# A hybrid decoder step on one core: the down product of two slices as seven chained rounds, ahead of the third

## The chip, the core and the metric

The kernel runs on one core of a Trainium2 chip. The core has a matrix engine (TensorE, PE in the profile, with its weight loads as PEld), VectorE (DVE), ScalarE (ACT), GpSimd (POOL) and SyncE (SP), which only issues transfers; POOL issues transfers too. The metric is the device time of one execution in microseconds (us).

## The reference

One inference step of a two-layer decoder over 1104 tokens (64 sampled, 16 meta, 1024 prompt tokens) of width 1024, all in float32. Layer 0 mixes with an mLSTM, layer 1 with an attention; behind each stands the same kind of feed-forward network:

```python
def swiglu(xn, w_gu, w_d):
    gu = xn @ w_gu
    return (jax.nn.silu(gu[..., :D_FF]) * gu[..., D_FF:]) @ w_d
...
        h = h + swiglu(rmsnorm(h, prm['norm_ffn'][l]), prm['w_gate_up'][l], prm['w_down'][l])
        if l == N_A_LAYERS - 1:
            shared = shared_kv(h, prm['norm_kv'], prm['w_kvf'], prm['b_fg_b'], prm['k_norm_b'])
    y = rmsnorm(h, prm['norm_final'])
```

`D_FF` is 2816. The change is in the last product, `@ w_d`, the down product, in both layers.

## The kernel before

**Tiling.** Activations lie with features on the 128 partitions and tokens along the free side. The 1104 tokens are three slices of 368 (`t` = 0, 1, 2). The residual is `H[t]`, 8 feature tiles of 128x368. The inner features are 22 tiles of 128 (`NF`), taken as 11 pairs (`NC`, `c`). Every float32 product is made of three matmuls: operands are split into a high part (a cast to fp32r on ScalarE) and a low part (a subtraction on VectorE), and high x high, high x low and low x high are summed in PSUM. `split` (L330 to L332) does a split.

**Gate and up.** `Unit` makes the gate (even `x`) or up (odd `x`) product of two feature tiles. `mark` (L1491, L1492) combines partial products from PSUM on VectorE; `out` multiplies silu(gate) by up (L1534) and sends each of the six results of an odd unit (two feature tiles, three slices) to DRAM, `hT[t]`, on SP (L1535). TensorE's order is written by hand here, that of the other engines is the scheduler's. The names `s1`, `c15`, `s2`, `e`, `t4`, `v2` are 128x368 columns in SBUF that hold an odd unit's results until they are sent.

**Down.** The last unit and the down product run with the orders of TensorE, VectorE and ScalarE written by hand; SP's and POOL's are the scheduler's. The product is a list of steps, `seq`: for each slice `t`, each half `z` of the output features (512 columns) and each pair `c`, one step of 24 matmuls of 128x368 (four output tiles `m`, two feature tiles, three products). Four PSUM banks (`dps`) hold the four outputs; behind the 11th pair they are added to `H[t]` (`add`, L1491).

A step needs a weight block (two tiles by 512 columns, 512 KB) and a pair of activations (368 KB). `w_load(i + 5)` fetches weights on SP into one of three raw buffers (`slots[0]`, `slots[1]`, `wr`), `w_split(i + 2)` splits them into one of four places (`slots[2 + i % 4]` and its low part). `h_load` fetches a pair from `hT` on POOL, through `flat[0]` and `flat[2]` at first and then through three buffers `hr`; `h_split` splits it into a place in the tiles `x0`, `x1`, `x2` and `T`, where it stays for the second half. `H[t]` itself is fetched back from DRAM (`hD`, 1472 KB) on POOL during the product, since its memory (`flat`, named `vA` in layer 0 and `Ht` in layer 1) is a buffer until then.

Behind a slice's outputs come squares (ScalarE) and their sum (`add_sq`, POOL L405, the last on VectorE), and then the norm: in layer 0 `norm_x`, which makes the inputs of the keys and values, in layer 1 `final`, the result. They are generators, taken a piece per step during the next slice's matmuls. Only slice 2's stands behind the last step. In layer 0 `first_values` then makes the first values, tile by tile.

Of the kernel before, what the change touches and what calls it, by code (L numbers as in the profile page):

```python
# [7 lines left out]
F32 = mybir.dt.float32  # L8
# [8 lines left out]
P = 128  # L17
D = 1024
KT = D // P
# [233 lines left out]
class Net:  # L253
# [139 lines left out]
    def add_sq(self, H, t, m, sp, x, late=KT - 1):  # L393
# [4 lines left out]
        if x == 0:  # L398
            self.sums[t] = self.ns[:, t % 2, :n]
            nc.scalar.activation(self.sums[t], H[t][:, m], AF.Square)  # L400
            return
# [77 lines left out]
    def mlp(self, H, w, l, heads=None, cb=None, early=None):  # L479
# [4 lines left out]
        self.sums = {}  # L484
# [3 lines left out]
        with self.pool(self.uid("nsp")) as sp, self.pool(self.uid("npp"), bufs=2, space=PSUM) as pn:  # L488
# [116 lines left out]
            with cw if not cb else ExitStack():  # L605
                def each(t, m):
                    if cb or t < 2 or m < KT - 2:
                        self.add_sq(H, t, m, sp, m)
# [5 lines left out]
                if cb:  # L614
                    def after(t):
                        nc.gpsimd.dma_start(self.hD[:, :, TS[t][0] : TS[t][1]], H[t])
                        return self.norm_x(H, t, None, sp, pn, psum=t < 2)
# [847 lines left out]
def ffn(self, H, flat, l, weights, order, mix, small, each, after, end, early=None):  # L1465
# [8 lines left out]
    hT = [self.dram.tile([P, NF, SL], F32, name=f"hT{l}_{t}") for t in range(3)]  # L1474
    with self.pool(f"ffn{l}") as fp, self.pool(f"ffnp{l}", space=PSUM) as pp:
# [19 lines left out]
        class Unit:  # L1495
# [34 lines left out]
            def out(u, c, i, t):  # L1530

                o = u.c[c]
                if u.odd:
                    tt(out=o, in0=o, in1=keep[t, i], op=ALU.mult)  # L1534
                    nc.sync.dma_start(hT[t][:, u.f + i], o)  # L1535
                else:
                    nc.scalar.activation(o, o, AF.Silu)
                    keep[t, i] = o

# [52 lines left out]
            def tail(u):  # L1592
# [15 lines left out]
        seq = [(t, z, c) for t in range(3) for z in range(2)  # L1608
               for c in ((*range(1, NC), 0) if (t, z) == (2, 1) else range(NC))]

        hseq = [i for i, (t, z, c) in enumerate(seq) if z == 0 or (t, c) == (2, 0)]
        hraw, hpart, wraw, wpart = {}, {}, {}, {}

        def h_load(j):
            if j < len(hseq):
                t, z, c = seq[hseq[j]]
                n = size[t]
                y, o = ((flat[0], 0), (flat[0], 2 * SL), (flat[2], 0), (flat[2], 2 * SL))[j] if j < 4 else (
                    self.ny(f"hr{l}_{j}"), 0)
                hraw[j] = y[:, o : o + 2 * n].rearrange("p (k n) -> p k n", k=2)  # L1620
                nc.gpsimd.dma_start(hraw[j], hT[t][:, 2 * c : 2 * c + 2])  # L1621

        def h_split(j):
            if j < len(hseq):
                t, z, c = seq[hseq[j]]
                x0, x1, x2 = (cut(self.flat_x[y], n) for y, n in ((0, 3), (1, 4), (2, 4)))
                a = [y for x in (2, 1, 4) for y in cut(Tx[x], 2)] + x2
                y = a[2] if z else [x0 + x1 + a[:4], a[4:] + x1 + a[:1], a[1:] + a[:1] + a[1:2]][t][c]
                hpart[t, c] = tuple(p[:, : 2 * size[t]].rearrange("p (k n) -> p k n", k=2) for p in y)
                self.split(hraw.pop(j), *hpart[t, c])  # L1630

        view = lambda y: y[:, : KT * P].rearrange("p (k n) -> p k n", k=2)

        def w_load(i):
            if i < len(seq):
                t, z, c = seq[i]
# [1210 lines left out]
```

## Time and profile before

| | us |
|---|---|
| median of 3 runs | 2843.36 (2842.17 to 2843.45) |
| profiled execution | 2841.83 |
| its span | 2840.1 |
| mean granted TensorE clock | 0.996 of full speed |

Each time below is from that one execution, counted from the start of its span. A row of the order of time has start, duration, engine, line, operation, output<-inputs and, in brackets, how long the engine had stood idle before it and what ended that. A row of busy time by stretch has the stretch, its length, the busy time (instructions) of PE, PEld, DVE, ACT and POOL, the granted clock, the busy share of the DMA engines and GB/s. Some matmul records are missing, so counts in a stretch can be a few per cent low.

### The profile page before, as it was taken

Reading aid. Unit: us, or ns where it says so; the run is one execution under the profiler, and the core shown is the slowest. Engines: PE = TensorE matmul, PEld = TensorE weight load, DVE = VectorE, ACT = ScalarE, POOL = GpSimd, SP = SyncE. Lnnn points to the kernel's source line nnn. Section 1 sums busy time; section 2 is a strip of 40 time slices with the busy share of each in tenths; the row PEclk is TensorE's granted clock in tenths of the full one; section 3 lists DMA queues with packets and bytes.
Section 4 is the critical chain, followed back from the end, with each engine's and each line's share of the span. In section 5 each row is a group of like instructions: output and inputs, shape, how many; then the busy total and the mean of one; then the engine's idle time right before and its main releaser. Section 6 shows DMA issues by size and latency. Waiting matters only on the chain. (4 is left out here: it accounts for less than half of the span.)

```text
span 2840.1 us, 54146 instructions
## 1 busy us (share of the span) xinstructions
PE 2773.6 (98%) x20630; PEld 2651.7 (93%) x20630; DVE 1743.6 (61%) x3606; ACT 1318.1 (46%) x2636; POOL 1085.0 (38%) x1582
## 2 busy tenths in 40 slices
PE   8999998999999999999999999999999999999999
PEld 7997988999999999999999888777999999999998
DVE  6144566687787755553466543777478777775553
ACT  6122464444444434443345444877344454443432
POOL 3042333066656411117572202555307666631210
PEclk9999999999999999999999999999999999999999
DMA  7156664122222275644453676442413222236653
GB/s 218 29 139 166 164 182 156 53 89 77 82 85 79 94 267 194 207 156 142 132 174 120 238 289 221 135 171 88 159 50 91 78 78 90 77 109 243 214 191 106
DMA packets 313974, 399.81 MB, mean 141 GB/s; under 512 B 28966, under 2 KB 235794, under 8 KB 312690
## 3 DMA queue, kind: packets, MB, share of 16 engines
q1 hardware_dynamic: 277282, 277.66, 30.8%
q0 software_dynamic: 35680, 118.12, 12.9%
q8 instruction: 162, 2.65, 0.4%
q14 instruction: 98, 0.80, 0.1%
q10 hardware_dynamic: 752, 0.57, 0.1%
HBM read 299.50 MB, written 96.77 MB: 140 GB/s over the span
## 5 line engine op out<-in xcount | busy, mean ns | idle before, releaser
L332 DVE TENSOR_TENSOR slot<-slot,slot 128x1024 fp32r<-128x1024 f32 (+3 forms) x263 | 252.6, 962 | 117.2 <-ACT slot L331 111.8
L331 ACT CAST slot<-slot 128x1024 fp32r<-128x1024 f32 (+3 forms) x263 | 206.5, 787 | 227.9 <-PE dps L270 95.9
L1515 PE MATMUL m<-x0h,slot 128*128 128x368 f32 x640 | 178.3, 329 | 0.0
L1515 PE MATMUL m<-x1h,slot 128*128 128x368 f32 x640 | 174.1, 331 | 2.7 <-DVE ns L1492 0.9
L1621 POOL DMA_DIRECT2D hr<-hT x60 | 32.5, 541 | 271.9 <-DVE T_2l L332 68.1
L111 POOL TENSOR_TENSOR slot<-vA 128x256 f32<-128x256 f32 x80 | 75.4, 952 | 149.8 <-DMA vA<-in_w_gate_up 77.6
L111 POOL TENSOR_TENSOR slot<-Ht 128x256 f32<-128x256 f32 x80 | 75.1, 949 | 150.3 <-DMA Ht<-in_w_gate_up 78.6
L1515 PE MATMUL m<-x2h,slot 128*128 128x368 f32 x480 | 132.3, 330 | 0.0
L332 DVE TENSOR_TENSOR slot<-Ht,slot 128x256 fp32r<-128x256 f32 (+3 forms) x101 | 88.1, 874 | 56.3 <-ACT slot L331 56.3
L332 DVE TENSOR_TENSOR slot<-vA,slot 128x256 fp32r<-128x256 f32 (+3 forms) x101 | 88.1, 874 | 55.4 <-ACT slot L331 55.4
L1515 PEld LDWEIGHTS m<-x1h,slot 128*128 128x128 f32 x640 | 115.6, 188 | 4.6 <-DVE vA L1491 1.5
L1515 PEld LDWEIGHTS m<-x0h,slot 128*128 128x128 f32 x640 | 116.1, 188 | 0.0
L405 POOL TENSOR_TENSOR ns<-ns,nq 128x368 f32<-128x368 f32 x50 | 56.6, 1133 | 142.5 <-ACT nq L403 136.5
L1515 PE MATMUL m<-x1l,slot 128*128 128x368 f32 x320 | 105.6, 330 | 0.0
L1515 PE MATMUL m<-x0l,slot 128*128 128x368 f32 x320 | 105.5, 330 | 0.0
L2641 ACT ACTIVATE s<-s,nb 128x272 f32<-128x272 f32 (+7 forms) x126 | 98.8, 786 | 0.0
L2676 ACT COPY th<-tp 128x768 f32<-128x768 f32 (+1 forms) x80 | 73.6, 921 | 47.4 <-PE tp L2668 25.8
L1515 PE MATMUL m<-T_2h,slot 128*128 128x368 f32 x320 | 93.8, 334 | 0.4 <-ACT vA L1521 0.4
L1515 PE MATMUL m<-T_4h,slot 128*128 128x368 f32 x320 | 93.7, 334 | 0.0
L326 DVE SCALAR_TENSOR_TENSOR slot<-slot,gain,slot 128x256 fp32r<-128x256 f32 (+2 forms) x152 | 63.7, 466 | 43.5 <-ACT slot L325 41.1
L332 DVE TENSOR_TENSOR slot<-wr,slot 128x1024 fp32r<-128x1024 f32 x42 | 53.5, 1274 | 60.0 <-ACT slot L331 60.0
L1515 PEld LDWEIGHTS m<-x2h,slot 128*128 128x128 f32 x480 | 86.9, 188 | 0.0
(867 smaller groups left out, 10362.3 us busy)
## 6 DMA issues: line engine op xcount, KB each, us to landing
slot<-in_w_down SPq DMA_DIRECT2D x88, 512.0 KB, 4.6
hr<-hT POOLq DMA_DIRECT2D x60, 368.0 KB, 5.4
wr<-in_w_down SPq DMA_DIRECT2D x42, 512.0 KB, 3.8
wraw<-in_w_in_a SPq DMA_DIRECT2D x40, 512.0 KB, 4.2
vA<-in_w_gate_up SPq DMA_DIRECT2D x40, 512.0 KB, 4.1
Ht<-in_w_gate_up SPq DMA_DIRECT2D x40, 512.0 KB, 4.2
kp<-in_cache_k SPq DMA_DIRECT2D x32, 512.0 KB, 5.9
vp<-in_cache_v SPq DMA_DIRECT2D x32, 512.0 KB, 8.4
```

The source lines that it names most:

```text
L111: self.net.nc.gpsimd.tensor_tensor(out=o, in0=a, in1=b, op=op)
L326: nc.vector.scalar_tensor_tensor(out=lo[:, k], in0=raw[:, k], scalar=gk, in1=hi[:, k].bitcast(F32), op0=ALU.mult, op1=ALU.subtract)
L331: self.nc.scalar.copy(hi, src)
L332: self.nc.vector.tensor_tensor(out=lo, in0=src, in1=hi.bitcast(F32), op=ALU.subtract)
L405: (nc.vector if x >= late else nc.gpsimd).tensor_tensor(out=s, in0=s, in1=sq, op=ALU.add)
L1515: nc.tensor.matmul(u.b[b][:, :SL], w[p][:, k], x[q][:, k], start=new and k == i == 0, stop=k == 1 and i == 2, skip_group_check=True)
L1621: nc.gpsimd.dma_start(hraw[j], hT[t][:, 2 * c : 2 * c + 2])
L2641: nc.scalar.activation(ss[z, u], ss[z, u], AF.Exp, bias=nb[:, z : z + 1], accum_out=sm[:, u, z : z + 1])
L2676: nc.scalar.copy(th.rearrange("p x z (u h q) -> p h (x z u) q", h=2, q=64)[:, :, :n], pt[:, :, :n])
```

## The change

Ten of the eleven pairs of slices 1 and 2 are taken as a two by two block product: the two slices are its columns, the two output halves its rows, and the first and second tile-group of the pairs (`h` = 0, 1) what is summed over. Seven products (`round_`) of five steps each take the place of eight. Their activations are `hA[1]` to `hA[7]`: 1, 2 and 4 are plain results of `out`, and 5, 6, 3 and 7 are made by `combine`, four sums per odd unit on VectorE. Their weights are plain for rounds 2, 3 and 6 (6 takes the sum that round 1 left) and sums on VectorE for 5, 1, 7 and 4 (`w_sum`, 20 per layer). Two weight halves are kept in the tiles `x1` and `x2` (`keep_w`, named `wx`). The first pair of slices 1 and 2 remains plain. The rounds are chained: an accumulator is added to several outputs, and the next round goes on in it. Then slice 0 follows with 22 plain steps, each activation pair split once for both halves, in reversed order for the second.

```diff
-    hT = [self.dram.tile([P, NF, SL], F32, name=f"hT{l}_{t}") for t in range(3)]
+    hT = [self.dram.tile([P, NF if t == 0 else 2, SL], F32, name=f"hT{l}_{t}") for t in range(3)]
+    hA = {r: self.dram.tile([P, NF // 2 - 1, SL], F32, name=f"hA{l}_{r}") for r in range(1, 8)}
...
-                    nc.sync.dma_start(hT[t][:, u.f + i], o)
+                    if t == 0:
+                        nc.sync.dma_start(hT[0][:, u.f + i], o)
+                    elif (t, i) != (2, 0):
+                        u.send({(1, 0): 1, (1, 1): 2, (2, 1): 4}[t, i], c)
...
+            def combine(u, part=None):
+
+                for r, o, i, j, f in (((5, "v2", "t4", "e", add),), ((6, "c15", "v2", "s2", sub), (3, "s1", "s1", "c15", sub)),
+                                      ((7, "e", "s2", "e", sub),))[part]:
+                    f(u.c[o], u.c[i], u.c[j])
+                    u.send(r, o)
...
+        def plain(t, z, lead):
+            step(("p", 0, z, 1), ("p", t, 0, 0), lead, (t, z))
+
+        round_(2, True)
+        plain(1, 0, False)
+        plain(2, 0, True)
+        round_(5, True, (2, 1))
+        round_(3, False)
+        plain(1, 1, False)
+        plain(2, 1, True)
+        round_(1, True, (1, 0))
+        round_(6, False, (1, 1))
+        round_(7, False, (2, 0), (2, 1))
+        round_(4, True, (2, 0))
...
+                if 3 <= i < 3 + NR:
+                    keep_w(1, i - 3, 0, 0)
+
+        def w_sum(i):
+            if i < len(ws) and ws[i][0] == "r":
+                _, r, q = ws[i]
+                if r == 5:
+                    sub(kept[1, q], wraw[i], kept[1, q])
+                    wraw[i] = kept[1, q]
+                elif r == 1:
+                    sub(kept[1, q], kept[2, q], kept[1, q])
+                elif r == 7:
+                    sub(wraw[i], kept[2, q], wraw[i])
+                elif r == 4:
+                    sub(wraw[i], wraw[i], kept[1, q])
...
+            for g in range(3):
+                u.combine(g)
...
+                k, todo = min(i + 2, len(seq) - 1), None
+                while wj < wneed[k]:
+                    wj += 1
+                    w_split(wj)
+                    todo = wj
+                while hj < hneed[k]:
+                    hj += 1
+                    h_split(hj)
+                    h_load(hj + 3)
+                if todo and not out:
+                    w_sum(todo + 1)
...
+                    for t, z in out:
+                        y = H[t][:, 4 * z + m]
+                        add(y, y, o)
...
+                if todo and out:
+                    w_sum(todo + 1)
+                if todo:
+                    w_load(todo + 3)
...
-    for t in range(3):
+    n = 0
+    for t in (1, 2, 0):
```

In `final` the slice that stands last is now slice 0, and the buffers of the results of slices 1 and 2 are new tiles.

**SP, at the start of the down product of layer 0.** Before, from the fourth weight block on (`slot` and `wr` are raw weight buffers, `hT` the sends of the last odd unit):

```order
L1638 DMA slot_4927<-in_w_down 128x2x512
L1535 DMA hT_1_5875<-vA_85 128x368
L1535 DMA hT_0_5874<-vA_83 128x368
L1535 DMA hT_2_5876<-nr_4921 128x368
L1535 DMA hT_0_5874<-vA_85 128x368
L1638 DMA slot_4928<-in_w_down 128x2x512
L1535 DMA hT_1_5875<-vA_85 128x368
L1535 DMA hT_2_5876<-vA_85 128x368
L1638 DMA wr_10025<-in_w_down 128x2x512
```

The same place now (`wx` are kept blocks; L1708 loads the block of the plain steps 5 and 6, the `wr` of the fourth row is step 3's):

```order
L1693 DMA wx_10177<-in_w_down 128x2x512
L1537 DMA hT_0_5874<-vA_85 128x368
L1693 DMA wx_10106<-in_w_down 128x2x512
L1545 DMA hA_1_5877<-vA_85 128x368
L1716 DMA wr_10102<-in_w_down 128x2x512
L1545 DMA hA_5_5881<-vA_83 128x368
L1545 DMA hA_6_5882<-vA_85 128x368
L1545 DMA hA_3_5879<-vA_85 128x368
L1545 DMA hA_7_5883<-vA_85 128x368
L1693 DMA wx_10106<-in_w_down 128x2x512
L1708 DMA slot_4928<-in_w_down 128x2x512
L1693 DMA wx_10106<-in_w_down 128x2x512
```

Kept blocks and the four combined sends now stand between the weight blocks of the first steps.

**POOL, at the same place.** Before (`hr` are pairs, `vA<-hD` the three slices of H, 83 to 85 for slice 0 to 2):

```order
L1621 DMA hr_6_10093<-hT_0_5874 128x736
L1851 DMA vA_83<-hD 128x8x368
L1621 DMA hr_7_10124<-hT_0_5874 128x736
L1851 DMA vA_84<-hD 128x8x368
L1621 DMA hr_8_10156<-hT_0_5874 128x736
L1621 DMA hr_9_10187<-hT_0_5874 128x736
L1851 DMA vA_85<-hD 128x8x368
```

Now (pair 5 and 6 are those of the plain steps 5 and 6):

```order
L1669 DMA hr_5_10114<-hT_1_5875 128x736
L1669 DMA hr_6_10150<-hT_2_5876 128x736
L1969 DMA vA_83<-hD 128x8x368
L1969 DMA vA_84<-hD 128x8x368
L1669 DMA hr_7_10184<-hA_5_5881 128x736
L1669 DMA hr_8_10216<-hA_5_5881 128x736
L1969 DMA vA_85<-hD 128x8x368
L1669 DMA hr_9_10247<-hA_5_5881 128x736
```

The three loads of H keep their places, but slices 1 and 2 are now added to in steps 5 and 6, where before slice 0 was the first, in step 10.

**VectorE, at the end of a group of rounds in layer 0.** Before, at the end of the first half of slice 0 (L1491 with `dps` adds an accumulator to H, L332 is the low part of a split):

```order
L332 TENSOR_TENSOR slot_4932<-wr_10025,slot_4931 128x1024
L1491 TENSOR_TENSOR vA_83<-vA_83,dps_10030 128x368
L1491 TENSOR_TENSOR vA_83<-vA_83,dps_10037 128x368
L1491 TENSOR_TENSOR vA_83<-vA_83,dps_10044 128x368
L1491 TENSOR_TENSOR vA_83<-vA_83,dps_10051 128x368
L332 TENSOR_TENSOR slot_4930<-slot_4927,slot_4929 128x1024
```

Now, where round 7 ends and round 4 begins (L1493 is a weight sum, L1492 an addition into H, x2 for two output halves):

```order
L1493 TENSOR_TENSOR slot_4928<-slot_4928,wx_10106 128x1024
L405 TENSOR_TENSOR ns_4920<-ns_4920,nq_10101 128x368
L332 TENSOR_TENSOR slot_4932<-slot_4928,slot_4931 128x1024
L332 TENSOR_TENSOR x0l_5421<-hr_33_11105,x0h_5420 128x736
L1492 TENSOR_TENSOR vA_85<-vA_85,dps_10745 128x368 x2
L1492 TENSOR_TENSOR vA_85<-vA_85,dps_10752 128x368 x2
L1492 TENSOR_TENSOR vA_85<-vA_85,dps_10759 128x368 x2
L1492 TENSOR_TENSOR vA_85<-vA_85,dps_10766 128x368 x2
L1493 TENSOR_TENSOR wr_10102<-wr_10102,wx_10106 128x1024
L332 TENSOR_TENSOR slot_4926<-wr_10102,slot_4925 128x1024
L332 TENSOR_TENSOR x0l_5421<-hr_34_11139,x0h_5420 128x736
```

A weight sum now stands directly ahead of the split of the same block, and eight additions where four stood.

189 lines of the change are left out of this document (122 added, 67 removed).

## The prediction

> **What bounds the kernel now.** I read the page's busy table first, then the busy time by stretch inside the down products (layer 0 from about 1000 to 1266, layer 1 from about 2560 to 2829).
>
> ```profile
> span 2840.1 us, 54146 instructions
> PE 2773.6 (98%) x20630; PEld 2651.7 (93%) x20630; DVE 1743.6 (61%) x3606; ACT 1318.1 (46%) x2636; POOL 1085.0 (38%) x1582
> ...
> core 0: us, PE busy (x) PEld busy (x) DVE busy (x) ACT busy (x) POOL busy (x), PEclk, DMA share, GB/s
> 1010.50:1095.10 84.60, 84.60 (x506) 84.60 (x505) 39.51 (x39) 32.28 (x39) 13.81 (x20) 1.00 0.62 215
> 1095.10:1179.00 83.90, 83.90 (x500) 83.66 (x500) 46.54 (x57) 38.87 (x51) 11.06 (x17) 1.00 0.55 184
> 2577.00:2660.00 83.00, 83.00 (x498) 83.00 (x496) 40.56 (x40) 34.27 (x40) 12.85 (x17) 1.00 0.56 188
> ```
>
> TensorE is busy 98% of the span, and in the three stretches inside the down products it is busy in every microsecond at a granted clock of 1.00, while VectorE works about half of the time. So each matmul taken out of these stretches is worth its interval, as long as nobody makes TensorE wait. The interval, from two rows of the order of time in TensorE (the first and the 25th matmul of one step, 24 apart):
>
> ```profile
> 1010.63 0.33 PE L269 MATMUL dps<-x1h,slot 128*128 128x368 f32 x1
> ...
> 1014.65 0.33 PE L269 MATMUL dps<-x1h,slot 128*128 128x368 f32 x1
> ```
>
> One row lasts 0.33 us, but they overlap: 4.02 us for 24, or 0.1675 us each. A step (one pair of weight tiles, four outputs, 24 matmuls) takes 4.02 us. The row at 1010.63 is step 3 of layer 0 (the first three pairs lie in x0, the fourth in x1), so step 0 began near 998.6.
>
> **Term 1, the matmuls.** Before: 3 slices x 2 halves x 11 pairs = 66 steps per layer. After: 7 rounds x 5 + 4 plain + 22 = 61. Five steps, 120 matmuls x 0.1675 = 20.1 us per layer, 40.2 us in both. That is all the change can give.
>
> **Term 2, the start of the rounds.** The stretch is already bound by transfers:
>
> ```profile
> 1005.00:1010.00 5.00, 5.00 (x32) 5.00 (x31) 1.63 (x2) 0.11 (x1) 1.44 (x2) 1.00 1.03 394
> 1010.00:1015.00 5.00, 5.00 (x32) 5.00 (x31) 2.06 (x2) 2.50 (x3) 0.55 (x1) 1.00 1.03 383
> 1030.00:1035.00 5.00, 5.00 (x32) 5.00 (x31) 2.75 (x3) 2.86 (x3) 0.54 (x1) 1.00 0.97 344
> 1040.00:1045.00 5.00, 5.00 (x31) 5.00 (x31) 3.55 (x6) 2.89 (x5) 1.43 (x2) 1.00 0.00 0
> ...
> 1009.89 1.05 ACT L331 CAST slot<-wr 128x1024 fp32r<-128x1024 f32 x1 [5.17 <-DMA wr<-in_w_down]
> 1010.97 1.23 DVE L332 TENSOR_TENSOR slot<-wr,slot 128x1024 fp32r<-128x1024 f32 x1 [4.34 <-ACT slot L331]
> 1012.12 0.92 DVE L332 TENSOR_TENSOR x1l<-hr,x1h 128x736 fp32r<-128x736 f32 x1
> ...
> vA<-hD POOLq DMA_DIRECT2D x6, 1472.0 KB, 9.6
> ```
>
> From 1005 to 1035 the DMA share is about 1 at some 385 GB/s, and only at 1040 is it idle. The cast of step 5's weights waits for its transfer; both low parts are ready at 1012.12 + 0.92 = 1013.0, and step 5 begins at 998.6 + 5 x 4.02 = 1018.7. So TensorE is about 5.7 us ahead of trouble there, and call it 5 for the whole stretch.
>
> Into this stretch the change puts five kept weight blocks (5 x 512 KB = 2.62 MB, read beside rounds 2 and 5) and three more sends of 184 KB (0.57 MB); one weight load goes, as the two plain steps share theirs (0.52 MB). Net 2.67 MB / 0.385 MB per us = 6.9 us. VectorE gets the last pair's four sums there:
>
> ```profile
> 1040.03 0.54 DVE L1491 TENSOR_TENSOR vA<-vA,dps 128x368 f32<-128x368 f32 x1 [4.40 <-PE dps L271]
> 1043.06 0.54 DVE L1491 TENSOR_TENSOR vA<-vA,dps 128x368 f32<-128x368 f32 x1 [0.48 <-PE dps L271]
> 1043.52 3.14 DVE L332 TENSOR_TENSOR slot<-slot,slot 128x1024 fp32r<-128x1024 f32 x2
> ```
>
> An operation of 128x368 lasts 0.54 us: four are 2.2, and the four additions into H, which now come in step 5 and not in step 10, are as much. They queue in VectorE behind the splits for two steps later, and the next steps need the accumulators that they read. Lateness: 6.9 + 2.2 + 2.2 - 5 = 6.3; I take **+6 us per layer**. Ends: 0 if the lead grows to 11 us, since a stall can't be less than nothing; 12 if the 1472 KB of H for slice 2, which has to wait for a pair buffer, also comes late (a rival below). On SP, the sends wait for VectorE's sums, and behind them stand the second kept block and the weights of step 5; on POOL, H of slice 2 stands behind two pair loads.
>
> **Term 3, the weight sums.** In rounds 5, 1, 7 and 4 each step has a new order: sum (VectorE), cast (ScalarE), low part of the weights, low part of the pair (VectorE), next sum. Each waits for the one before it:
>
> ```profile
> 1014.15 1.05 ACT L331 CAST slot<-slot 128x1024 fp32r<-128x1024 f32 x1 [2.50 <-DMA slot<-in_w_down]
> 1015.23 1.23 DVE L332 TENSOR_TENSOR slot<-slot,slot 128x1024 fp32r<-128x1024 f32 x1 [2.20 <-ACT slot L331]
> 1016.38 0.92 DVE L332 TENSOR_TENSOR x1l<-hr,x1h 128x736 fp32r<-128x736 f32 x1
> ...
> 1044.54 2.96 POOL L405 TENSOR_TENSOR ns<-ns,nq 128x368 f32<-128x368 f32 x2 [1.37 <-ACT nq L403]
> ```
>
> No row shows the f32 sum of 128x1024. Nearest is the split's subtraction of that size (1.23 us); bounds are the 736 columns of the pair (0.92) and the pair of splits beside POOL's additions (3.14 / 2 = 1.57). I take 1.23, as the size is the same. Then: sum to cast 1.23 + 0.06, cast to low part 1015.23 - 1014.15 = 1.08, low part to the next 1.15, that to the sum 0.9 (0.92 with a little overlap): 4.4 us against TensorE's 4.02. With idle time of VectorE inside it, a step is 0.35 us too slow: rounds 5 and 1 are five steps each and followed by rounds without sums, which let it recover (0). Rounds 7 and 4 follow one another: ten steps, 3.5 us. Within them come the additions of round 6's end (4) and of round 7's end (8, two per accumulator); the rows at 1043.06 and 1043.52 are 0.46 apart: 12 x 0.46 = 5.5. POOL's additions of slice 1's squares fall into the same steps, and VectorE lost 3.14 - 2 x 1.15 = 0.84 us beside them; six times 0.75 is 4.5. Sum 13.5. There are four buffers for split weights, and a split writes the one that TensorE left four weights ago, so VectorE can be two steps (8 us) ahead when round 7 begins: 5.5, so **+6 us per layer**, mostly between round 7 and round 4, where TensorE needs accumulators whose additions stand behind splits. Ends: 1 (POOL's additions fall into VectorE's idle time, sums of 0.92) and 10 (the lead is one step).
>
> **Term 4, the clock.** What a stall costs beyond itself stands in the gate/up product:
>
> ```profile
> 599.49 0.56 PE L1515 MATMUL m<-U_6h,slot 128*128 128x368 f32 x1 [1.98 <-DVE vA L1491]
> ...
> 596.00:600.00 4.00, 2.02 (x11) 1.71 (x11) 4.00 (x7) 2.68 (x5) 3.92 (x5) 0.96 0.55 167
> 600.00:604.00 4.00, 4.00 (x18) 4.00 (x16) 4.00 (x3) 0.00 (x0) 4.00 (x4) 0.62 0.45 131
> 604.00:608.00 4.00, 4.00 (x25) 4.00 (x25) 2.25 (x5) 1.00 (x3) 2.72 (x3) 1.00 0.01 2
> ```
>
> After a wait of 1.98 us the clock was 0.62 over the next 4 us, 18 matmuls and not 24 or 25: (1 - 0.62) x 4 = 1.5 us lost. Terms 2 and 3 hold one such stall each: **+3 us per layer** (0 if they come as many short ones, 5 if there are three). The Trainium skill, page "TensorE: Matmul & The Clock Gate", section "Part 1: The HAM clock gate", says that the clock is halved after at least one idle window of about 3.4 us; by that rule stalls of 2 or 3 us cost nothing more, and the time would be 6 us lower. The rows above do not agree with so long a window, and the sum goes by them.
>
> **Term 5, gate and up.** The four sums of each odd unit (40 per layer) and three more sends lie beside matmuls:
>
> ```profile
> 804.00:844.80 40.80, 40.80 (x245) 40.53 (x244) 32.25 (x52) 19.81 (x42) 24.97 (x25) 1.00 0.26 80
> ...
> 726.70 0.54 DVE L1492 TENSOR_TENSOR ns<-m,ns 128x368 f32<-128x368 f32 x1
> 727.92 0.54 DVE L1491 TENSOR_TENSOR ns<-m,ns 128x368 f32<-128x368 f32 x1 [0.68 <-PE m L1515]
> ...
> L1534 DVE TENSOR_TENSOR Ht<-Ht,Ht 128x368 f32<-128x368 f32 x18 | 15.5, 862 | 0.0
> ```
>
> Two units take 40.8 us, of which VectorE works 32.25. Four sums are 2.2 us alone and 3.4 at the 862 ns that such products take beside POOL, so it stays under 36. Two of them stand ahead of the subtraction at 726.70 that frees a bank: it comes 0.9 us later, and VectorE waited 0.68 us for TensorE after it. So up to 0.2 us per even unit: **+1 us per layer** (0 to 4). Sends: 80 GB/s leave room.
>
> Nothing else is on the path: ScalarE's 8 more casts per layer have room (32.28 of 84.60 us busy). The slices' new order at the end leaves the same number of tiles and transposes behind the last step (0, within 1 us either way); the values start with slice 1, whose norm was done earlier, just as slice 0's was.
>
> **Sum.** Per layer -20.1 + 6 + 6 + 3 + 1 = -4.1; both -8.2. The profiled execution took 2841.83 us (span 2840.1 and 1.7 around it), the median of the three runs is 1.5 above it: 2833.6 beside the profile, **2835.2** as a median.
>
> **The rivals.**
> 1. *All is hidden.* Terms 2 to 4 at their lower ends (0, 1, 0), gate/up 1: 2 x (-20.1 + 2) = -36, 2807. For it: VectorE works only 40 to 47 of 84 us in the down product, and a lead of 5 us exists in the worst stretch. Against: the DMA share of 1.03 and the chain of 4.4 us. 17%.
> 2. *The losses eat the gain, and no more.* Each layer loses 17 to 23 us: 2838 to 2849. It needs 4 us more than the forecast in each layer, for instance VectorE one step less ahead at round 7 (term 3 at 10). 28%.
> 3. *Slower: H of slice 2.* Its transfer stands in POOL behind two pair loads, of which the second needs the buffer that step 5's split frees. In the forecast that split ends near 1019, and at the 9.6 us above H lands near 1029, for an addition due at 998.6 + 6.25 x 4.02 = 1023.7. If it lands after 1036, TensorE stands 7 us longer and has another cold clock: 1.5. Then -4.1 + 8.5 = 4.4 per layer, 2852. It decides from about 1036 on. For it: three loads of H and the kept blocks share one saturated DMA. Against: the 9.6 us. 17%.
> 4. *The change does not do what it says*: excluded, as 240 matmuls fewer stand in TensorE's order (17001 rows and 16761).
>
> **How the numbers follow.** Forecast (2825 to 2837.6) 38%; rival 1 17%, rival 2 28%, rival 3 17%. A measurement of this kernel can tell about 0.2%, 5.7 us, from no change. Faster by more: 38 + 17 = 55%; within: 28%; slower: 17%. The range 2813 to 2853 leaves out half of rival 1 and a part of rival 3. The forecast's own range is 2825 to 2838.
>
> **What would show it.** Term 1: 240 matmuls fewer, and a down product that takes about 5 us less in each layer than its 66 x 4.02 = 265 us, not 20 less. Term 2: TensorE waits for VectorE's additions or low parts in steps 5 to 7, and the DMA share is 1 for over 40 us. Term 3: a wait for an addition between rounds 7 and 4, 3 to 6 us. Term 4: granted clock under 0.8 behind both. Term 5: waits in the gate/up product grow by no more than a few us. No waits there would make terms 2 and 3 wrong and give rival 1; a wait of 8 us or more around step 6, until H of slice 2 lands, gives rival 3; a gate/up product that is longer by over 5 us in a layer would make term 5 wrong.

## The result, and the profile after

| | us |
|---|---|
| before, median | 2843.36 (2841.98 to 2846.22) |
| after, median | 2860.11 (2855.64 to 2863.41) |
| ratio | 1.0058 (95% interval 1.0043 to 1.0073) |
| profiled execution of after; its span | 2863.41; 2861.7 |

The change makes the kernel slower, by 0.58% or some 17 us. The page's first lines:

```profile
span 2861.7 us, 54039 instructions
...
PE 2755.9 (96%) x20390; PEld 2621.2 (92%) x20390; DVE 1869.1 (65%) x3790; ACT 1317.8 (46%) x2652; POOL 1105.6 (39%) x1612
```

TensorE has 240 instructions fewer and is busy for 17.7 us less, but the span is 21.6 us longer: TensorE's idle time has grown by more than its work has shrunk. To see where, both spans are cut at the same places of the program (first matmul of gate/up, first and last of the down product, per layer) and read as busy time by stretch. Before:

```profile
589.50:998.50 409.00, 405.19 (x2401) 401.91 (x2400) 321.19 (x504) 197.51 (x401) 243.38 (x234) 1.00 0.27 85
998.50:1265.80 267.30, 267.30 (x1591) 266.82 (x1590) 147.09 (x176) 110.78 (x148) 38.33 (x57) 1.00 0.60 203
1265.80:2147.80 882.00, 865.91 (x8749) 779.85 (x8748) 500.83 (x1635) 462.66 (x994) 355.25 (x751) 1.00 0.48 161
2147.80:2556.60 408.80, 405.12 (x2402) 402.06 (x2401) 318.66 (x503) 196.97 (x401) 242.21 (x233) 1.00 0.27 85
2556.60:2828.70 272.10, 272.10 (x1646) 271.92 (x1646) 132.22 (x139) 99.28 (x120) 38.93 (x50) 1.00 0.56 191
```

After:

```profile
593.10:1005.30 412.20, 408.38 (x2401) 401.39 (x2401) 341.83 (x540) 194.10 (x399) 242.21 (x234) 1.00 0.31 96
1005.30:1275.00 269.70, 252.40 (x1470) 249.45 (x1469) 187.21 (x227) 111.80 (x152) 49.36 (x68) 0.98 0.63 209
1275.00:2163.70 888.70, 868.39 (x8750) 781.87 (x8748) 503.52 (x1640) 464.42 (x1000) 355.60 (x754) 0.99 0.48 160
2163.70:2575.60 411.90, 407.91 (x2401) 401.45 (x2401) 338.02 (x539) 194.82 (x399) 241.43 (x233) 1.00 0.30 97
2575.60:2848.50 272.90, 257.63 (x1527) 255.66 (x1526) 174.24 (x195) 101.84 (x128) 50.19 (x65) 0.97 0.60 199
```

The third number of a row is the length. Gate/up: +3.2 and +3.1. Down product: +2.4 and +0.8, where 120 fewer matmuls were to give -20.1 us each. Between the layers: +6.7; behind the last product (11.4, now 13.2): +1.8. The remaining 3.6 (589.5, now 593.1) lie ahead of the first changed instruction. That point moves from one execution to the next (in the runs below it lies between 588.3 and 597.4), so it is no effect of the change.

The down products lose 22.5 and 20.9 us inside, and the waits of TensorE show at which places. The order of time in TensorE, layer 0:

```profile
1036.59 0.65 PE L1949 MATMUL dps<-T_2h,slot 128*128 128x368 f32 x1 [6.94 <-DVE vA L1492]
1133.99 0.41 PE L1949 MATMUL dps<-x0h,slot 128*128 128x368 f32 x1 [1.83 <-DVE vA L1492]
1159.67 0.65 PE L1949 MATMUL dps<-x0h,slot 128*128 128x368 f32 x1 [5.27 <-DVE vA L1492]
1228.83 0.41 PE L1949 MATMUL dps<-x0h,slot 128*128 128x368 f32 x1 [2.10 <-DVE vA L1492]
1280.41 0.89 PE L413 MATMUL nps<-ns,ones 128*128 128x368 f32 x2 [2.47 <-DVE ns L405]
1298.35 0.39 PE L269 MATMUL tmps<-slot,x0h 128*128 128x256 f32 x1 [3.07 <-ACT vf L2054]
```

Two groups of the view of waits (total, times, longest), `vA` for layer 0 and `Ht` for layer 1:

```profile
PE dps L1949 <- DVE vA L1492: 16.6, 6, 6.9
PE dps L1949 <- DVE Ht L1492: 14.3, 5, 6.1
```

1036 is step 6 (the additions of the plain step 5 are late), 1134 the start of round 7, 1160 the start of round 4, 1229 the change of halves in slice 0, and the two rows that follow belong to the last norm and the first values. Before, none of these waits was over 0.3 us. From the gaps between the starts of matmuls (0.1675 us each where nothing waits), in us:

| | layer 0 | layer 1 | predicted per layer |
|---|---|---|---|
| matmuls (term 1) | -20.1 | -20.1 | -20.1 |
| waits at the start of the rounds (term 2) | 7.9 | 8.4 | 6 |
| waits at rounds 7 and 4 (term 3) | 7.4 | 8.3 | 6 |
| low clock behind these (term 4) | 3.2 | 4.4 | 3 |
| waits in the slice-0 part | 3.8 | 0 | 0 |
| gate/up (term 5) | 3.2 | 3.1 | 1 |
| behind the down product | 6.7 | 1.8 | 0 |

### The profile page after: what moved, and what is told of

Read it like the earlier page. It is cut to its first block, busy times and chain, and to the rows that moved or that the text cites. A ratio compares the mean times of both kernels' runs of the same rounds, so it can differ in the third digit from the quotient of the medians.

```text
span 2861.7 us, 54039 instructions
## 1 busy us (share of the span) xinstructions
PE 2755.9 (96%) x20390; PEld 2621.2 (92%) x20390; DVE 1869.1 (65%) x3790; ACT 1317.8 (46%) x2652; POOL 1105.6 (39%) x1612
## 5 line engine op out<-in xcount | busy, mean ns | idle before, releaser
L1949 PE MATMUL dps<-x0h,slot 128*128 128x368 f32 x1440 | 366.7, 334 | 19.0 <-DVE vA L1492 9.7
L1949 PEld LDWEIGHTS dps<-x0h,slot 128*128 128x128 f32 x1440 | 258.9, 190 | 22.4 <-issue 21.0
L332 DVE TENSOR_TENSOR slot<-slot,slot 128x256 fp32r<-128x256 f32 (+2 forms) x233 | 211.2, 908 | 68.3 <-ACT slot L331 63.5
L331 ACT CAST slot<-slot 128x256 fp32r<-128x256 f32 (+2 forms) x233 | 175.0, 754 | 163.7 <-PE m L1516 66.8
L1949 PE MATMUL dps<-x0l,slot 128*128 128x368 f32 x720 | 239.1, 332 | 1.0 <-DVE x0l L332 1.0
L1516 PE MATMUL m<-x1h,slot 128*128 128x368 f32 x640 | 180.0, 335 | 3.3 <-DVE ns L1493 0.9
L1949 PEld LDWEIGHTS dps<-x0l,slot 128*128 128x128 f32 x720 | 136.7, 190 | 1.3 <-DVE x0l L332 1.2
L332 DVE TENSOR_TENSOR slot<-Ht,slot 128x256 fp32r<-128x256 f32 (+3 forms) x101 | 91.5, 907 | 52.3 <-ACT slot L331 52.3
L332 DVE TENSOR_TENSOR slot<-vA,slot 128x256 fp32r<-128x256 f32 (+3 forms) x101 | 92.1, 913 | 50.3 <-ACT slot L331 50.3
L1669 POOL DMA_DIRECT2D hr<-hA x62 | 33.7, 543 | 217.6 <-DVE x0l L332 177.8
L405 POOL TENSOR_TENSOR ns<-ns,nq 128x368 f32<-128x368 f32 x50 | 63.1, 1262 | 129.7 <-ACT nq L403 125.0
```

The source lines that it names most:

```text
L331: self.nc.scalar.copy(hi, src)
L332: self.nc.vector.tensor_tensor(out=lo, in0=src, in1=hi.bitcast(F32), op=ALU.subtract)
L405: (nc.vector if x >= late else nc.gpsimd).tensor_tensor(out=s, in0=s, in1=sq, op=ALU.add)
L1516: nc.tensor.matmul(u.b[b][:, :SL], w[p][:, k], x[q][:, k], start=new and k == i == 0, stop=k == 1 and i == 2, skip_group_check=True)
L1669: nc.gpsimd.dma_start(hraw[j], src)
L1949: nc.tensor.matmul(o, w[:, k, ms], a[:, k], start=lead and k == x == 0, stop=k == 1 and x == 2, skip_group_check=True)
```

## The experiments

Each ratio is to before, with its 95% interval. Layer 0's times are quoted; layer 1 shows the same unless it is said.

**The start of the rounds.** VectorE and ScalarE in the changed kernel, in order of time:

```profile
1025.93 1.23 DVE L332 TENSOR_TENSOR slot<-wx,slot 128x1024 fp32r<-128x1024 f32 x1 [0.36 <-ACT slot L331]
1035.07 0.92 DVE L332 TENSOR_TENSOR x0l<-hr,x0h 128x736 fp32r<-128x736 f32 x1 [7.91 <-ACT x0h L331]
1035.91 1.42 DVE L1492 TENSOR_TENSOR vA<-vA,dps 128x368 f32<-128x368 f32 x3
...
1034.23 0.80 ACT L331 CAST x0h<-hr 128x736 fp32r<-128x736 f32 x1 [8.33 <-DMA hr<-hA]
```

The busy time by stretch (the last three numbers of a row are the granted clock, the DMA share and GB/s):

```profile
985.00:990.00 5.00, 5.00 (x32) 5.00 (x31) 2.34 (x4) 2.10 (x5) 0.00 (x0) 1.00 0.00 0
1030.00:1035.00 5.00, 0.00 (x0) 0.00 (x0) 0.00 (x0) 0.77 (x1) 0.00 (x0) 0.84 1.03 383
1035.00:1040.00 5.00, 3.41 (x11) 3.44 (x12) 3.85 (x6) 1.01 (x3) 0.54 (x1) 0.50 1.04 389
```

TensorE waits for additions (1035.91). These stand in VectorE's order behind the low part of pair 7 (1035.07), which stands behind the cast of it, which waits until 1034.2 for the transfer. The DMA share is 1.03 in the stretch, while it was 0.00 from 985 to 990. Pair 7 had been issued at 1018.1, behind two loads of H.

*e1: H of slice 0 loaded later.*

```diff
-                y, o = ((flat[0], 0), (flat[0], 2 * SL), (flat[2], 0), (flat[2], 2 * SL))[j] if j < 4 else (
+                y, o = ((flat[0], 0), (flat[0], 2 * SL), (flat[2], 0), (flat[2], 2 * SL), (flat[0], 0))[min(j, 4)] if j < 4 or j == 20 else (
-                if i in (1, 3, 8):
-                    y = {1: 1, 3: 2, 8: 0}[i]
+                if i in (1, 3, 20):
+                    y = {1: 1, 3: 2, 20: 0}[i]
```

> Edit: the residual H of slice 0 is loaded some twenty steps later in each layer (its place in memory holds pair 20 of the rounds until then); nothing else. In the changed kernel TensorE waits 6.9 us in layer 0 and 5.7 us in layer 1 at the start of round 5 until pair 7 (the first of round 5) is there, with another 1.7 us of low clock behind it. Theory B (bytes): too much is moved in this stretch, whatever the order; 1.47 MB less at 0.385 MB per us is 3.8 us less per layer: a wait of about 3 us, 2852. Theory Q (queue): pair 7 stands on POOL's queue behind two loads of H and shares the DMA with SP's; here the loads of H for slices 1 and 2 stand ahead of it, as many bytes as before: waits as they are, 2860 (2857 to 2863).

2864.65 us, ratio 1.0084 (1.0066 to 1.0101). The wait is 6.4 (layer 1: 5.4), and 0.6 and 1.0 us of new waits stand ahead of it. 1.47 MB less, and nothing gained. That alone does not refute theory B, since POOL's order of time shows that the run changes a second thing:

```profile
1021.18 0.89 POOL L1969 DMA_DIRECT2D vA<-hD  x1 [10.50 <-DMA hA<-vA]
```

This is the load of H of slice 2. It now stands ahead of pair 7 and waits 10.5 us for a send. So pair 7 is issued 18.0 us behind the first step, not 12.8. It is then 12.6 us in flight, not 16.1: with fewer bytes beside it the transfer was shorter, but its later issue took the gain back.

*e2: also H of slice 2 later.* Pair 7 was put in the place of H of slice 2, but the load of H stands ahead of pair 7's split in the program, so round 5 works on the wrong pair.

> Edit: as e1, and pair 7 is loaded into the place of H of slice 2, which so can be loaded only when pair 7 is split; one load of H stands ahead of pair 7 and not two. Theory Q: pair 7 lands 1.47 MB at half the rate, some 7 us, earlier; the wait at the start of round 5 and its low clock go, 8.7 us per layer: 2843. Theory B: H of slice 2 is still needed in the same stretch, so the wait stays at 3 us as in e1: 2852. Beside both: H of slice 2 comes later than in the changed kernel; if it lands behind step 6, VectorE waits there for it and TensorE some microseconds later.

2866.28 us, ratio 1.0093 (1.0076 to 1.0110). It doesn't decide between the theories; e5 takes its place.

*e5: pairs 7 and 8 early, H of slice 0 behind them.*

```diff
-                y, o = ((flat[0], 0), (flat[0], 2 * SL), (flat[2], 0), (flat[2], 2 * SL))[j] if j < 4 else (
+                y, o = ((flat[0], 0), (flat[0], 2 * SL), (flat[2], 0), (flat[2], 2 * SL))[j] if j < 4 else (flat[0], (2 * j - 10) * SL) if j in (7, 8) else (
```

> Edit: pairs 7 and 8 (the first two of round 5) are loaded into free columns of the place of H of slice 0, ahead of the loads of H; H of slice 0 so comes after both are split. Theory Q (the pair's place in POOL's queue): pair 7 is there before step 5, the wait of 6.9 us (layer 1: 5.7) and its 1.7 us of low clock go: 2843. Theory B (too many bytes in this stretch): the pairs come in time, but H of slice 1, due at the end of step 5, now stands behind them; 1.47 MB (3.8 us) less are moved before it, so about 3 us of the wait stay, for an addition into H: 2850 to 2853.

2862.59 us, ratio 1.0076 (1.0060 to 1.0092). The one wait has become six of 4.8 us in all. The two longest in TensorE, and a row of VectorE ahead of the first, in order of time:

```profile
1035.74 0.40 PE L1949 MATMUL dps<-T_2h,slot 128*128 128x368 f32 x1 [2.01 <-DVE vA L1492]
1060.48 0.43 PE L1949 MATMUL dps<-x0l,slot 128*128 128x368 f32 x1 [0.95 <-DVE x0l L332]
...
1030.67 1.23 DVE L1493 TENSOR_TENSOR wx<-wr,wx 128x1024 f32<-128x1024 f32 x1 [4.47 <-DMA wr<-in_w_down]
```

So the place of pair 7 is not the whole cause either: with it in time, VectorE waits for a block of weights, ahead of the same additions.

*e6: gate/up without the four sums.*

```diff
                     for r, o, i, j, f in (((5, "v2", "t4", "e", add),), ((6, "c15", "v2", "s2", sub), (3, "s1", "s1", "c15", sub)),
                                           ((7, "e", "s2", "e", sub),))[part]:
-                        f(u.c[o], u.c[i], u.c[j])
                         u.send(r, o)
```

> Edit: the four activation sums of each odd unit are left out, their sends are kept (rounds 3, 5, 6 and 7 then work on activations that are not summed). In the changed kernel the gate/up product is 3.2 us longer in layer 0 and about 3 in layer 1 than before, in steps of 0.3 us. If VectorE's sums are the cause: both go, 2854 (2853 to 2856). If the three more sends are: 2860. If the difference is that between two executions: gate/up stays within 1 us of the changed kernel's, 2860.

2857.54 us, ratio 1.0065 (1.0044 to 1.0085), not apart from that of the change. Gate/up takes 409.2 and 409.0 us, as before the change: VectorE's sums cost the 3 us, the additional sends nothing. But the time does not follow. The rounds start 3 us earlier, and a new wait of 5.1 us (layer 1: 6.4) stands in them, on a weight block that lands late:

```profile
1013.19 1.04 ACT L331 CAST slot<-wr 128x1024 fp32r<-128x1024 f32 x1 [19.56 <-DMA wr<-in_w_down]
...
1015.00 0.68 PE L1948 MATMUL dps<-x0h,slot 128*128 128x368 f32 x1 [5.11 <-ACT x0h L331]
```

The rows are of ScalarE and of TensorE, in order of time. Here the transfers decide when the rounds get on, not the end of gate/up.

**Rounds 7 and 4.** VectorE and (last row) POOL in the changed kernel, in order of time, beside round 7:

```profile
1143.89 2.02 DVE L1493 TENSOR_TENSOR wr<-wx,wr 128x1024 f32<-128x1024 f32 x1
1147.10 1.23 DVE L332 TENSOR_TENSOR slot<-wr,slot 128x1024 fp32r<-128x1024 f32 x1 [1.19 <-ACT slot L331]
1148.24 0.92 DVE L332 TENSOR_TENSOR x0l<-hr,x0h 128x736 fp32r<-128x736 f32 x1
1149.08 2.01 DVE L1493 TENSOR_TENSOR slot<-slot,wx 128x1024 f32<-128x1024 f32 x1
1152.20 1.23 DVE L332 TENSOR_TENSOR slot<-slot,slot 128x1024 fp32r<-128x1024 f32 x1 [1.12 <-ACT slot L331]
...
1148.33 1.67 POOL L405 TENSOR_TENSOR ns<-ns,nq 128x368 f32<-128x368 f32 x1 [2.16 <-ACT nq L403]
```

The sum (L1493) takes 2.0 us beside POOL's addition of squares; then VectorE idles 1.2 us until ScalarE has cast it; then the two low parts. A step is 5.1 us, against TensorE's 4.02.

*e3: the squares later.*

```diff
-                    for _ in range(1 if i < NX else 2):
+                    for _ in range(0 if i < NX else 2):
                         if pend:
```

> Edit: the squares of slices 1 and 2 (ScalarE, and POOL's additions of them) begin with the slice-0 part, no longer beside rounds 1, 6, 7 and 4. In the changed kernel TensorE waits 1.8 and 5.3 us (layer 1: 1.9 and 6.1) at the start of round 7 and of round 4, with 1.5 to 2.4 us of low clock behind. Theory C (contention): the weight sums take 2.0 us beside POOL's additions and 1.22 without; four of them are on VectorE's path: 3.2 us, VectorE's own addition of 0.5, and some of the low clock: 4 to 5 us less per layer, 2851. Theory L (latency): VectorE idles 1.2 us in each step for ScalarE's cast between the sum and the low part, and this sets the step's length; shorter sums help by 3 us at most, and the squares cost as much in the slice-0 part, where the norms alternate between VectorE and ScalarE: 2857 to 2862.

2857.85 us, ratio 1.0064 (1.0047 to 1.0081). Without POOL beside them the sums take 1.22 us, and a step 4.4 (VectorE in order of time):

```profile
1141.37 1.22 DVE L1493 TENSOR_TENSOR wr<-wx,wr 128x1024 f32<-128x1024 f32 x1
...
1145.75 1.22 DVE L1493 TENSOR_TENSOR slot<-slot,wx 128x1024 f32<-128x1024 f32 x1
```

The two waits shrink from 7.1 to 3.9 us, as theory C has it (3.2 us), but in layer 0 a norm is then late, as theory L warned; its group among TensorE's waits, none in the changed kernel:

```profile
PE nps L413 <- DVE x1l L428: 5.5, 1, 5.5
```

Both are right about one half.

*e4: the sums one step further ahead.*

```diff
+        def w_sums(i):
+            for j, rs in ((i + 1, (5,)), (i + 2, (1, 7, 4))):
+                if j < len(ws) and ws[j][0] == "r" and ws[j][1] in rs:
+                    w_sum(j)
...
-                    w_sum(todo + 1)
+                    w_sums(todo)
```

> Edit: the weight sums of rounds 1, 7 and 4 stand one step further ahead in VectorE's order (two weights ahead of the split, not one), so that ScalarE casts one sum while VectorE makes the next. Theory L: a step of VectorE in rounds 7 and 4 falls from 4.4 (5.1 beside POOL) by the idle 1.2 us to 3.3 (4.1): the waits of 1.8 and 5.3 us shrink to 2 in sum and the low clock goes: 7 us less per layer, 2846. Theory C: the contended sums remain, four times 0.8 us: 3 to 4 us per layer stay, 2852. If the order costs nothing at all (the additions alone make the waits): 2860.

2845.38 us, ratio 1.0012 (1.0002 to 1.0021). Sums and low parts now stand back to back in VectorE's order of time:

```profile
1153.03 1.21 DVE L332 TENSOR_TENSOR slot<-slot,slot 128x1024 fp32r<-128x1024 f32 x1
1154.16 0.91 DVE L332 TENSOR_TENSOR x0l<-hr,x0h 128x736 fp32r<-128x736 f32 x1
1155.00 1.21 DVE L1493 TENSOR_TENSOR wr<-wr,wx 128x1024 f32<-128x1024 f32 x1
```

Of the waits at rounds 7 and 4 only 1.5 us is left in layer 0 and nothing in layer 1. Theory L predicted the time to a microsecond: the order of instructions, not their number, made this loss.

*e11: no sums in rounds 7 and 4.*

```diff
                 elif r == 7:
-                    sub(wraw[i], kept[2, q], wraw[i])
+                    pass
                 elif r == 4:
-                    sub(wraw[i], wraw[i], kept[1, q])
+                    pass
```

> Edit: of the changed kernel: the ten weight sums of rounds 7 and 4 are left out (these rounds then work on single weight blocks), nothing else. Theory L and C alike: the waits at the start of rounds 7 and 4 (1.8 and 5.3 us, in layer 1 1.9 and 6.1) shrink to what the 12 additions alone make, 2 us at most, and the low clock goes: 2844 to 2847, as in e4. If the additions make the waits and the sums fit beside them: no change, 2860.

2840.84 us, ratio 1.0004 (0.9993 to 1.0014). Both waits are gone; the 12 additions alone make none. e4, with all its sums, stands 0.08% above it, less than the intervals tell apart, so its order hides nearly all of them.

**The slice-0 part and the norm.** VectorE and (last two rows) ScalarE in the changed kernel, in order of time, one step:

```profile
1247.58 1.23 DVE L332 TENSOR_TENSOR slot<-slot,slot 128x1024 fp32r<-128x1024 f32 x1 [1.48 <-ACT slot L331]
...
1249.17 0.54 DVE L425 TENSOR_TENSOR npy<-vA,nr 128x368 f32<-128x368 f32 x1
1250.24 0.54 DVE L428 TENSOR_TENSOR x2l<-npy,x2h 128x368 fp32r<-128x368 f32 x1 [0.53 <-ACT x2h L426]
1250.70 0.54 DVE L425 TENSOR_TENSOR npy<-vA,nr 128x368 f32<-128x368 f32 x1
1252.72 1.23 DVE L332 TENSOR_TENSOR slot<-slot,slot 128x1024 fp32r<-128x1024 f32 x1 [1.48 <-ACT slot L331]
...
1249.74 0.47 ACT L426 CAST x2h<-npy 128x368 fp32r<-128x368 f32 x1 [2.20 <-DVE npy L425]
1251.64 1.05 ACT L331 CAST slot<-slot 128x1024 fp32r<-128x1024 f32 x1
```

VectorE is idle for 2.0 us (1.48 and 0.53) of each 5.14 us, ScalarE for 2.2 ahead of one cast alone: product, cast, low part, product, cast, and only then the cast of the next weights. The splits fall behind TensorE, so raw buffers come free late, and the weights of the values with them: their loads begin at 1262.7, before the change at 1246.0.

*e7: e4, and the norm's cast a step behind its product.*

```diff
-            nc.scalar.copy(xh[:, k], y)
             yield
+            nc.scalar.copy(xh[:, k], y)
...
-                for _ in range(0 if i < NX else 1 if i < NX + NC else 2):
+                for _ in range(0 if i < NX else 1):
```

> Edit: e4, and beside it in the slice-0 part: the norm of slices 1 and 2 makes VectorE's product one step before ScalarE's cast of it, and one piece of it stands in each step (not two in the second half). In e4 VectorE and ScalarE wait for one another there, 5.1 us a step against TensorE's 4.0; behind it in layer 0 TensorE waits 2.1 us at the change of halves, 0.7 near the end, 3.4 for the last norm, and 1.9 when the values begin. Theory N (this alternation is the cause, through the late loads of the values' weights): 6 to 8 us less in layer 0, nothing in layer 1: 2838. Rival (the values begin with another slice, whose rows are sent late; the alternation is hidden by the lead): the last two waits stay, 5.3 us: 2843.

2833.98 us, ratio 0.9975 (0.9965 to 0.9984). The waits at the change of halves and near the end are gone, that of the last norm falls from 3.4 in e4 to 0.7, and the loads of the values' weights begin at 1242.8. The last wait stays at 2.0, so the rival holds for this one. Against e4 the time falls by 0.37%, some 10 us, of which these waits show 5.4. This gain stands in the medians of ten runs each. The two profiled executions don't show it: from the first matmul of gate/up to the end both take 2247 us, as other waits are longer in that of e7 (2.9 us for 1.5 ahead of round 4, 7.2 for 6.4 at the start). Where the rest lies is open.

**All together, and the start again.**

*e8: e7, e5, and the first plain step of slice 2 ahead of round 4.*

```diff
...
         round_(2, True)
-        plain(1, 0, False)
-        plain(2, 0, True)
+        plain(1, 0, False, (1, 0))
...
-        round_(4, True, (2, 0))
+        plain(2, 0, True)
+        round_(4, False, (2, 0))
```

> Edit: e7 and e5 together, and the first plain step of slice 2 stands between rounds 7 and 4, in round 4's accumulators (one load of weights more, four additions fewer, and no additions into H of slice 2 before the end of round 5). If the waits found are all there is beside the 20.1 us of matmuls: 2838 (e7's expectation) - 17 (e5) - 2 (additions) = 2819, 0.8% below before. If bytes hold the start back (theory B): 2826. If H of slice 2 or the additional weights make a new wait: 2830 or more.

2831.93 us, ratio 0.9973 (0.9961 to 0.9985), no better than e7 by the intervals. The wait between rounds 7 and 4 is down to 0.2 us, but at the start TensorE waits 6.4 us as ever.

*e9: also the plain steps of the second half ahead of round 5.*

```diff
         plain(1, 0, False, (1, 0))
-        round_(5, True, (2, 1))
-        round_(3, False)
-        plain(1, 1, False, (1, 1))
+        plain(1, 1, True, (1, 1))
         plain(2, 1, True, (2, 1))
+        round_(5, True, (2, 1))
+        round_(3, False, (1, 1))
...
-                if 3 <= i < 3 + NR:
-                    keep_w(1, i - 3, 0, 0)
+                if 5 <= i < 5 + NR:
+                    keep_w(1, i - 5, 0, 0)
```

> Edit: e8, and the two plain steps of half 1 (slices 1 and 2) stand right behind the first one, ahead of round 5; the kept blocks of round 5 are loaded two weights later. Two steps are put ahead of round 5 that need one load of weights between them and no pair of their own, so round 5's weights, kept blocks and pairs fall due 8 us later. In e8 the wait at the end of step 5 is 6.4 us in layer 0 and 6.0 in layer 1, with 1.7 us of low clock. Theory B (bytes: the DMA is full from 1005 to 1050, and what falls due at this place comes late whatever its order): the wait goes in both layers, 16 us: 2816. Theory V (VectorE's order: the additions into H stand behind the split of round 5's second weights; the DMA is only full because much is prefetched): the additions of three plain steps stand there now in place of one, so the wait stays at 5 us or more: 2830.

2837.32 us, ratio 0.9985 (0.9973 to 0.9997). 8 us more time for the transfers, and the wait is 7.1 us. VectorE's order of time shows why:

```profile
1029.89 1.22 DVE L1493 TENSOR_TENSOR wx<-wr,wx 128x1024 f32<-128x1024 f32 x1 [6.11 <-DMA wr<-in_w_down]
1031.87 1.87 DVE L1492 TENSOR_TENSOR vA<-vA,dps 128x368 f32<-128x368 f32 x4
```

From 1023.8 to 1029.9 it waits for a block that is wanted two steps later, with the ready additions behind it.

*e10: e9, the activation sums spread one, one and two.*

```diff
-                for r, o, i, j, f in (((5, "v2", "t4", "e", add),), ((6, "c15", "v2", "s2", sub), (3, "s1", "s1", "c15", sub)),
-                                      ((7, "e", "s2", "e", sub),))[part]:
+                for r, o, i, j, f in (((5, "v2", "t4", "e", add),), ((6, "c15", "v2", "s2", sub),),
+                                      ((3, "s1", "s1", "c15", sub), (7, "e", "s2", "e", sub)))[part]:
```

> Edit: e9, and of the four activation sums the second of the pair stands a quarter of a unit later (one, one and two, in place of one, two and one). In e8 the gate/up product takes 411.6 us in layer 0 (before: 408.5; without the sums, in e6: 407.7). If it is the pair of sums ahead of the subtraction that frees a bank which costs 0.3 us for every two units: 2 to 3 us less per layer, about 5 below e9. If VectorE is simply short of time there: as e9 within 1.5 us.

2835.53 us, ratio 0.9984 (0.9976 to 0.9993): as e9. Gate/up takes 413.0 us (e9: 411.6). Which instruction delays TensorE there is open.

*e12: e9, the first sum of round 5 behind the additions.*

```diff
-                if j < len(ws) and ws[j][0] == "r" and ws[j][1] in rs:
+                if j < len(ws) and ws[j][0] == "r" and ws[j][1] in rs and ws[j] != ("r", 5, 0):
                     w_sum(j)
...
         def w_split(i):
             if i < len(ws):
+                if ws[i] == ("r", 5, 0):
+                    w_sum(i)
```

> Edit: e9, and the first weight sum of round 5 stands directly ahead of its split, behind the additions of the first plain step (in e9 ahead of them: VectorE waited there 6.1 us, to 1029.9, for a block of weights that was 14 us in flight, while the additions for which TensorE waited 7.1 us were ready). Theory V: the wait at 1032 shrinks from 7.1 to 2 us or less and the low clock goes; the sum is needed only for step 8, two steps later: 6 us per layer less than e9, 2825 where e9 gives 2837. Theory B: the transfers decide; the additions are made, and TensorE waits as long a step or two later: as e9 within 3 us.

*e13: e12, H of slice 2 loaded once pair 6 is split* (pair 6 lies in its place until then):

```diff
...
-                if i in (1, 3, 8):
-                    y = {1: 1, 3: 2, 8: 0}[i]
+                if i in (1, 5, 8):
+                    y = {1: 1, 5: 2, 8: 0}[i]
```

> Edit: e12, and H of slice 2 (1.47 MB) is loaded only when pair 6 is split, some 10 us later, ahead of its first addition in step 7; pair 6 lies in its place until then. Theory V: what was to be had is had with e12; the same time within 2 us, or a few us more where the additions of step 7 now wait for H. Theory B: the first weights of round 5 land 1.47 / 0.385 = 3.8 us earlier; what is left of the wait in e12 shrinks by up to 4 us per layer.

e12: 2831.09 us, ratio 0.9962 (0.9949 to 0.9975). e13: 2827.53 us, ratio 0.9947 (0.9933 to 0.9961). The order of time in TensorE, the large waits at the start; first in e12:

```profile
1025.84 0.41 PE L1956 MATMUL dps<-T_2h,slot 128*128 128x368 f32 x1 [0.95 <-DVE vA L1492]
1034.73 0.65 PE L1956 MATMUL dps<-T_2h,slot 128*128 128x368 f32 x1 [4.68 <-DVE vA L1492]
```

The same in e13:

```profile
1035.18 0.58 PE L1956 MATMUL dps<-T_2h,slot 128*128 128x368 f32 x1 [2.58 <-DVE vA L1492]
```

With one more of 0.3 us in each, the 8.7 us of waits in e9 (7.1 and 1.5) become 6.0 and then 2.9 (layer 1: 6.0, 5.4 and 2.9). In e12 the wait moves one plain step on, to the next additions behind the same sum; theory V holds for 2.7 us of it (layer 1: 0.6), theory B for the 3.1 us that e13 takes away (2.5). Both are at work: a late transfer, and ready work behind the instruction that waits for it. e13 is the fastest version run, 0.53% under before; the intervals do not tell it from e12.

## Why the prediction was wrong

It said 2835.2 (2813 to 2853), 55% for faster; the time is 2860.1, slower than all its cases.

- **Term 1** was right: 20.1 us per layer went, and TensorE's busy time fell.
- **Term 2** (6 us, found 7.9 and 8.4) had place and cause right, waits for additions in steps 5 to 7 with a full DMA, and was somewhat small. It took the lateness as a sum of bytes over rate. In e1 and e5, which take bytes away ahead of the wait, it does not shrink by their time, as the transfers that are left change their places; e12 shows that VectorE's fixed order adds its part.
- **Term 3** (6 us, found 7.4 and 8.3): its chain of 4.4 us is what e3 shows, with the sum at 1.22 us for the estimated 1.23. What POOL adds was taken as 0.75 us in six steps, and is 0.8 in four, which makes the sum 12.2 and not 13.5. Mis-sized was the lead, "VectorE can be two steps (8 us) ahead": the waits of 1.8 at round 7 and 5.3 at round 4 leave about 5 us for it.
- **Term 4** (3 us, found 3.2 and 4.4) had the size right, in part by luck: the waits of 7 and 5 us cost 1.5 to 1.7 us each (layer 1: 2.8 behind 6.1), but that of 1.8 us cost nothing. The length of a stall, from which the term was made, does not decide it (below).
- **Term 5** (1 us, found 3.2 and 3.1): mis-sized, and within its ends. e6 shows VectorE's sums as the cause.
- **"Nothing else is on the path"** is the step that failed. The norms of two slices now stand beside slice 0's matmuls alone, and the text gave their order 0 us. TensorE lost 3.8 us within layer 0's slice-0 part, and 5.3 us of the 6.7 between the layers are the late last norm (2.5, before 0.3) and the values (3.1). e7 removes most of these waits by the order of cast and product. The other 1.4 us between the layers are less than that stretch differs between executions (882 us in e12, 888 in e13, which are alike there). The 1.8 us behind the last product were not tested; slice 0, which now ends last, has rows of two outputs, so eight sends stand on SP there where six stood.

Together, against the forecast of -8.2 us: terms 2 to 4 cost 9.6 more in the two layers (39.6 for 30), term 5 4.3, the slice-0 part and what lies behind the products 12.3. That makes +18.0, and with the 3.6 ahead of the first change the 21.6 by which the two profiles differ. By the medians it is 16.7.

Of the rivals, "slower: H of slice 2" came nearest in place (a wait of 7 us at step 6), by another mechanism: TensorE waited for pair 7. H of slice 2 was late too, beyond the rival's 1036: issued at 1022.5, it landed at 1041.3, but its additions stood behind pair 8's split and began only at 1042.1. The chances were wrong in kind: three losses were each taken at the middle of their bounds, and nothing was kept for places that no term names, though the change gives VectorE 184 instructions more and moves two norms.

## What to carry to other kernels

Taking work off the busiest engine pays only as far as the fixed orders of the others keep pace: here seven products for eight cost 0.6% as they came, and gained 0.5% once the orders around them were changed. Where two engines hand a tile back and forth within a step (sum, cast, low part), put the first of them one step ahead; that alone took the ratio from 1.0058 to 1.0012. An instruction that waits for a prefetch belongs behind every ready one that another engine waits for, and when a full transfer queue is suspected, take one transfer away and look whether the wait shrinks or only moves, and whether the other transfers kept their places.

## What the hardware showed

A 128x1024 float32 subtraction in VectorE took 1.22 us, and 2.0 us when POOL added 128x368 beside it, whose own 0.98 us (1275.4) became 1.67. The sum at 1149.08 lost 0.8 us, about as long as the two overlapped (POOL's addition ended at 1150.0). The Trainium skill, page "GPSIMD Engine Reference", section "2. Architecture", says that the two share a memory port; the rows fit that, and give its price.

How long TensorE stands still did not alone decide the clock behind it. In the changed kernel the clock was 0.54 for 4 us behind the wait of 6.9 us (14 matmuls, not 24), and stayed at 1.00 behind that of 1.83. But the 1.98 us of before was followed by 0.62, 2.58 us in e13 by 0.57 and 2.88 us in e7 (at 1154.4) by 1.00. The Trainium skill's rule (page "TensorE: Matmul & The Clock Gate", section "Part 1: The HAM clock gate") speaks of a window of some 3.4 us that runs freely, whatever the kernel does. The traces agree with such a window: in all 15 the granted clock is 1.00 or 0.50 and nothing between, and it changes only at points that lie a whole number of 3.413 us apart. Busy time by stretch, each from one such point to the next, around the wait of 1.83 us in the changed kernel (first row) and that of 2.58 us in e13:

```profile
1132.35:1135.76 3.41, 1.77 (x11) 1.80 (x12) 3.41 (x7) 0.00 (x0) 0.83 (x2) 1.00 0.63 176
...
1031.84:1035.25 3.41, 0.83 (x6) 0.56 (x4) 2.72 (x4) 1.36 (x2) 0.00 (x0) 1.00 1.02 384
1035.25:1038.66 3.41, 3.41 (x12) 3.41 (x13) 2.26 (x4) 1.04 (x2) 0.00 (x0) 0.50 1.04 384
```

What they do not agree with is that the whole window must be idle, as the prediction read that rule. TensorE was idle for 1.64 us of the first stretch, and the clock stayed at 1.00; it was idle for 2.58 us of the second, and the clock was 0.50 in the next. The 2.88 us of e7 fell into two stretches, 1.71 and 1.17 us, and cost nothing. In the 15 traces, every stretch of gate/up and down matmuls at full clock with 1.90 us or more idle was followed by half the clock, and none with less than 1.86 us was. So at lengths of about 2 to 3.8 us a wait's place in time decides whether it costs another 1.5 to 1.7 us.
